# A two-layer hybrid attention trunk: the input projection with pairs of half-precision numbers in place of pairs of rounded single-precision ones

## The chip, the cores and the metric

One core of a Trainium2 chip runs the whole kernel in one launch. The metric is device time in microseconds (us). The matmul engine is called PE (PEld is its loading of weights), VectorE is DVE, ScalarE is ACT, GpSimd is POOL, and SP is the engine that issues most DMAs; DVE, ACT and POOL also work on the data between the matmuls. Each engine runs its instructions in order and waits for other engines by semaphores.

## What is computed

Two layers act on 512 latent tokens and 256 context tokens of 1024 features. Each layer normalizes and modulates its input (scale and shift come from a small projection of `c`), multiplies it by one wide matrix `w_in`, and takes ten pieces from the product:

```python
hx = _rmsnorm(x, norm_g) * (1.0 + scale_x) + shift_x
px = hx @ w_in                       # 1024 -> 5376 columns
a_k, a_v, b_k, b_v, a_q, b_q, a_z, b_z, g_a, g_b = _split(px, SPLIT_SIZES)
# widths      512  512  128  128  512  512  512  512 1024 1024
a_att = _na_latent(rmsnorm(a_q), rmsnorm(a_k), a_v, context k and v, rpb)  # neighbourhood attention
b_att = grouped attention of rope(rmsnorm(b_q)), rope(rmsnorm(b_k)), b_v
o_a = (a_att * silu(a_z)) @ w_o_a ;  o_b = (b_att * silu(b_z)) @ w_o_b
x = x + gate_x * ((sigmoid(g_a) * o_a + sigmoid(g_b) * o_b) @ w_out)
```

The norms of q and k go over heads of 64 columns and add `EPS` to the mean of squares. The context passes through the same weights in layer 0; in layer 1 only its k and v are needed. All data are float32. The change touches `hx @ w_in` and what scales its ten pieces.

## The kernel before

**Products of pairs.** A float32 matmul is made of three. Each factor is split into a high half, rounded to the format `fp32r` (4 bytes an element), and a low half, the rest; `mm3` (line 431) adds hi·hi, hi·lo and lo·hi in PSUM. The weights are split when they are loaded. `load_w` (395) takes 512 columns in eight raw tiles of 128 rows: for each an SP DMA of 256 KB into one of three "raw" buffers, a cast by ACT (403) into a "whi" buffer, and a subtraction (406) by POOL or DVE into a "wlo" buffer; there are eight buffers of each kind, and for AQ and half of BQ some of the attention's own. `load_w2` (410) does the same for 256 columns, with two blocks of 128 rows in a tile, so four tiles (cast 418, subtraction 420). `mix_lo` and `bq_lo` (425, 426) say whose the subtraction is: `mix_lo` gives POOL the even tiles and DVE the odd ones. So a tile's cast waits only for its own DMA, and its subtraction only for its cast. The input `hx` lies turned (features on the partitions) as hi and lo, made by `start_mod` (374) for layer 0 and `make_hx`/`turn_hx` (324, 335) for layer 1, during layer 0's output projection.

**Order of the work.** A layer is written as a sequence of stages, and PE follows that order: AK, AV and AQ (`tok_proj`, 443: tokens on the partitions, eight steps of three matmuls of 128x512 for each of six or four blocks of 128 tokens); then neighbourhood attention, head by head; then BKV (256 columns) and BQ; grouped attention; the branches' products with `w_o_a` and `w_o_b` and their merge; the output projection (1205 to 1240). The remaining projections (`a_z`, `b_z`, `g_a`, `g_b`) are cut into twelve chunks of 256 columns (`fill_chunks`, 607; `chan_proj`, 450: features on the partitions). Their loads and pieces are put between the heads of the attentions (`pipeline`, 997), where PE would wait for the softmax, two loads ahead of their use (`in_order`, 630). What a chunk gives is evacuated by ACT's tanh (614), DVE's product for silu (616), and partly spilled to memory by DMA (618). A stage's weights are loaded and split while the stage before computes; the framework's scheduler settles each engine's order from the dependences and the order of the program.

**Evacuation.** `evac_na` (543) squares and sums a block by heads (`head_ss`, 497, with `EPS` in an extra column that `open_heads`, 490, writes), takes the power -1/2 on POOL (`head_pow`, 503), multiplies, and `turn` (520) transposes the result on PE a little later. Transposes go to PSUM buffers of kind "t", of which there are two. `evac_va` (558) splits V again. `head_out` (789) and `divide` (806) add the two halves of an attention's output and multiply it by the silu gate. `stage_q` (849) lays a head's queries out in the attention's own "qs" buffers.

Of the kernel before, what the change touches and what calls it, by code (L numbers as in the profile page):

```python
# [44 lines left out]
XB, RX = 6, 2  # L45

# [24 lines left out]
def hybrid_kernel(es: ExitStack, tc, x, ctx, cvec, w_ada, w_ada0, small, gvec, w_in, w_o_a, w_o_b, w_out,  # L71
# [72 lines left out]
    hx0 = [[big("hx") for _ in range(2)] for _ in range(2)]  # L144
# [26 lines left out]
    def raw_tile():  # L171
        return wp.tile([128, 512], F32, tag="raw", name=nm("raw"), bufs=3)
# [134 lines left out]
    def ada_mod(l):  # L307
        mod_finish(l, ada_sum(0, 16, 2).rearrange("p (a k) v -> p a k v", a=2), 0, 8)

# [25 lines left out]
    def turn_hx(l, t, y, h, hx, pool):  # L335

        v = 0 if t < 4 else 1
        full = pool.tile([128, 4, 128], F32, tag="half", name=nm("half"), bufs=2)
        pt = psw(512, "t")
        for k in range(4):  # L340
            T.transpose(pt[:, 128 * k:128 * k + 128], y[:, 512 * h + 128 * k:512 * h + 128 * k + 128], ident)
        for k in range(4):
            kk = 4 * h + k
            S.activation(full[:, k, :], pt[:, 128 * k:128 * k + 128], AF.Identity,
                         bias=modc[:, l, v, kk:kk + 1], scale=modc[:, l, v, 8 + kk:9 + kk])
        hi = hx[0][h].rearrange("p (k n) -> p k n", k=4)[:, :, 128 * t:128 * t + 128]
        lo = hx[1][h].rearrange("p (k n) -> p k n", k=4)[:, :, 128 * t:128 * t + 128]
        V.tensor_copy(R(hi), full)
        V.tensor_tensor(R(lo), full, hi, ALU.subtract)
# [34 lines left out]

    def split_hi(raw):
        hi = wp.tile([128, 512], F32R, tag="whi", name=nm("whi"), bufs=8)
        S.copy(hi, raw)
        return hi

    def split_lo(raw, hi, eng):  # L390
        lo = wp.tile([128, 512], F32R, tag="wlo", name=nm("wlo"), bufs=8)
        eng.tensor_tensor(lo, raw, F(hi), ALU.subtract)
        return hi, lo

    def load_w(src, col0, n, nk, lo_eng, k0=0, own=None, bufs=8):

        pool, x = (wp, "") if own is None else (own, "x")
        res = []
        for k in range(k0, k0 + nk):
            raw = raw_tile()  # L400
            nc.sync.dma_start(raw[:, :n], src[128 * k:128 * k + 128, col0:col0 + n])
            hi = pool.tile([128, 512], F32R, tag="whi" + x, name=nm("whi"), bufs=bufs)
            S.copy(hi[:, :n], raw[:, :n])  # L403
            lo = pool.tile([128, 512], F32R, tag="wlo" + x, name=nm("wlo"), bufs=bufs)
            e = lo_eng(k)
            e.tensor_tensor(lo[:, :n], raw[:, :n], F(hi[:, :n]), ALU.subtract)  # L406
            res.append((hi, lo))
        return res

    def load_w2(src, col0, nk, lo_eng):  # L410

        res = []
        for i in range(nk // 2):
            raw = raw_tile()
            nc.sync.dma_start(raw.rearrange("p (k n) -> p k n", k=2),
                              src[256 * i:256 * i + 256, col0:col0 + 256].rearrange("(k p) n -> p k n", k=2))
            hi = wp.tile([128, 512], F32R, tag="whi", name=nm("whi"), bufs=8)
            S.copy(hi, raw)  # L418
            lo = wp.tile([128, 512], F32R, tag="wlo", name=nm("wlo"), bufs=8)
            lo_eng(i).tensor_tensor(lo, raw, F(hi), ALU.subtract)  # L420
            res += [(hi[:, c:c + 256], lo[:, c:c + 256]) for c in (0, 256)]
        return res

# [4 lines left out]
    def hx_k(hx, part, k):  # L428
        return hx[part][k // 4].rearrange("p (k n) -> p k n", k=4)[:, k % 4, :]
# [6 lines left out]

    def tok_mm(ps, w, n, a, t, k0, k1):
        for k in range(k0, k1):
            hi, lo = a(0, k), a(1, k)
            mm3(ps, (R(hi[:, 128 * t:128 * t + 128]), R(lo[:, 128 * t:128 * t + 128])),  # L440
                (w[k][0][:, :n], w[k][1][:, :n]), k == 0, k == KT - 1)
# [8 lines left out]
    def chan_proj(w, f, a, n0, n1, evac, late=0):  # L450


        ps = psw(n1 - n0)
        nk = len(w)
        wh = lambda k, i: w[k][i][:, 128 * f:128 * f + 128]
        act = lambda k, i: R(a(i, k)[:, n0:n1])
# [9 lines left out]
    hp = {"late": [], "lag": 0}  # L466

# [22 lines left out]
    def open_heads(stack, name, bufs):  # L490

        hp["p"] = stack.enter_context(tc.tile_pool(name=name, bufs=bufs, reuse_waits="tile"))
        hp["sq"] = [hp["p"].tile([128, 8, HD + 1], F32, name=nm("sq"), bufs=1) for _ in range(2)]
        for sq in hp["sq"]:
            V.memset(sq[:, :, HD:HD + 1], HD * EPS)

# [87 lines left out]
    def layer(l, hx, nxt, start):  # L584
# [3 lines left out]
        a_hx = lambda part, k: hx_k(hx, part, k)  # L588
# [17 lines left out]

        def fill_chunks(col0, dst, spill, silu, eng):

            def evac(f, n0, n1, ps):
# [4 lines left out]
                S.activation(d, ps, AF.Tanh, scale=0.5)  # L614
                if silu:
                    V.scalar_tensor_tensor(d, d, 1.0, ps, ALU.add, ALU.mult)
                if spill is not None:
                    (nc.sync if not first else G if silu else S).dma_start(spill[:, f, n0:n1], d)
            res = []
            for i in range(2):  # L620
                st = {}

                def ld(i=i, st=st):
                    st["w"] = load_w2(W, col0 + 256 * i, KT, eng)
                res.append((ld, [lambda f=f, n0=n0, n1=n1, i=i, st=st:
                                 chan_proj(st["w"], f, a_hx, n0, n1, lambda f, a, b, ps: evac(2 * i + f, a, b, ps))
                                 for f in range(2) for n0, n1 in spans]))
            return res
# [64 lines left out]

        bgp_es = ExitStack()
# [25 lines left out]
        else:  # L720
            open_heads(bgp_es, f"cp{l}", 1)
            w = load_w(W, C_AK, 512, KT, mix_lo)
# [18 lines left out]
        w = load_w(W, C_AQ, 512, KT, mix_lo, own=hp["p"])  # L741
# [17 lines left out]
        if True:  # L759
# [29 lines left out]
            def head_out(po, e, dst, eng=None):  # L789
# [3 lines left out]
                t1 = att["p"].tile([128, 512], F32, tag="ho", name=nm("ho"), bufs=1)  # L793
                a = t1[m:m + 64, :n]
                S.copy(a, po[o:o + 64, :n])
                V.tensor_tensor(a, po[m:m + 64, :n], a, ALU.add)
# [52 lines left out]
            def stage_q(src, e):  # L849

                n = 768 if first else 512
                qs = att["p"].tile([128, n], F32R, tag=f"qs{e}", name=nm("qs"), bufs=1)
# [35 lines left out]
            def ctx_values(p, vsl, dst, e, back=None):  # L888
# [18 lines left out]
                head_out(po, e, dst)  # L907
# [7 lines left out]
            def open_att(name, width, n_p, n_t):  # L915
# [3 lines left out]
                att["turn"], att["spare"] = 0, False  # L919
# [10 lines left out]
            V.memset(bedg[64:128, 0:128], NEG)  # L930

# [36 lines left out]
            def na_values(h, ps_):  # L968
# [25 lines left out]
                head_out(po, e, zv[64 * e:64 * e + 64, h // 2, 0:512], V if h == 7 else G)  # L994
# [21 lines left out]
            akt = [k_tile(e, True) for e in range(2)]  # L1016

# [8 lines left out]
            def values_of(dst, f, back=None):  # L1026
                def g(h, st):
                    vsl = f(h, st[0])
                    if first:
                        e = h % 2  # L1030
                        zv = dst.rearrange("p (f n) -> p f n", f=4)
                        ctx_values(st[1], vsl, zv[64 * e:64 * e + 64, h // 2, 512:768], e, back)
# [39 lines left out]
            def split_vb():  # L1072
                shrink(vf.rearrange("p t n -> p (t n)"), vs, vbig[:, 2946:2948], vbig[0:1, 2948:2949])
                v = vf.rearrange("p t (h d) -> p (t h) d", h=2)
                d = vb.rearrange("p t h q d -> p (t h) q d")
                S.activation(d[:, :, 0, :], v, AF.Copy, scale=vs[:, 0:1])
# [4 lines left out]
            w = load_w2(W, C_BKV, KT, mix_lo)  # L1081
            w_q = load_w(W, C_BQ, 512, 4, bq_lo) + load_w(W, C_BQ, 512, 4, bq_lo, 4, hp["p"], 4)
# [11 lines left out]
            def evac_bq(t, ps):  # L1094
# [3 lines left out]
                else:  # L1098
                    rope_heads(4, ps, rs, gbc[:, 0, :], None, qbv, t)
            for t in range(qt):  # L1100
# [19 lines left out]
            lift = vbig[:, 2950:2951].to_broadcast([128, 768])  # L1120

# [15 lines left out]
            def gq_values(h, st):  # L1137
# [6 lines left out]
                divide(psw(512, "t"), r, e, dst, vs[:, 1:2])  # L1144
# [30 lines left out]
            pipeline(fill, 8, gq_first, values_of(zb, gq_values, vs[:, 1:2]), early, bg)  # L1175
            gq_es.close()

        with tc.tile_pool(name=f"mrg{l}", bufs=1, reuse_waits="tile") as mp:
# [37 lines left out]
            for n in range(2):  # L1216
# [200 lines left out]
    hx1 = []  # L1417

    def nxt():
        if not hx1:  # L1420
            hx1.extend([[big("hx") for _ in range(2)] for _ in range(2)])
# [78 lines left out]
```

## Time and profile before

| | us |
|---|---|
| median of 3 runs (lowest, highest) | 1127.27 (1126.77, 1128.93) |
| the profiled execution | 1127.56 |
| its span, first to last instruction | 1125.6 |
| granted TensorE clock over the span | 0.993 |
| PE busy, 5826 instruction records | 1093.3 |
| ACT busy | 579.0 |
| DVE busy | 774.7 |
| POOL busy | 490.6 |

The spans of the stages, read from the timeline (us from the start of the span; edges to a few us, since a stage's evacuation runs into the next):

| | start and AK | AV | AQ | neighb. att. | BKV, BQ | grouped att. | merge | out |
|---|---|---|---|---|---|---|---|---|
| layer 0 | 0-63 | 63-102 | 102-133 | 133-306 | 306-382 | 382-550 | 550-592 | 592-659 |
| layer 1 | 659-692 | 692-727 | 727-753 | 753-881 | 881-938 | 938-1050 | 1050-1075 | 1075-1126 |

How to read the rows that follow: a group's row gives the line, engine and operation, out<-in by the program's names, the shape (partitions x elements) and type, how often, busy us and the mean ns of one, and the idle time of the engine ahead of them with what ended it. A timeline row gives start and duration in us. PE's matmuls are pipelined: a duration holds the way through the array too, and consecutive starts are closer together than durations.

### The profile page before, as it was taken

To read this page: it belongs to the slowest core of one execution; us is meant where nothing else is said; L and a number is where in the kernel's file an instruction comes from. 1 tells how busy PE (TensorE), PEld (TensorE's weight loads), DVE (VectorE), ACT (ScalarE), POOL (GpSimd) and SP (SyncE) were. 2 spreads that over 40 slices of the span, in tenths; PEclk is the share of its full clock that TensorE was granted. 3 is DMA by queue.
4 is the path that set the end of the run, shared out by engine and by line. 5 is a ranking of instruction groups with operands and counts; after the bars stand their busy time and mean duration, and the time that the engine had idled before them with its cause. 6 is when DMAs were issued, how large, how long until landed. Compare 5 with 4: busy or idle time off the path is not lost.

```text
span 1125.6 us, 16862 instructions
## 1 busy us (share of the span) xinstructions
PE 1093.3 (97%) x5826; PEld 905.3 (80%) x5826; DVE 774.7 (69%) x1492; ACT 579.0 (51%) x1154; POOL 490.6 (44%) x405
## 2 busy tenths in 40 slices
PE   8999999999999999979999999999999999999998
PEld 5688888888998877757788888888888987776677
DVE  4666788897466477776577785458878765677473
ACT  6453266665433576755330284326666446776431
POOL 1054254654247144454521545235554563563531
PEclk9999999999999999989999999999999999999999
DMA  9454322242351488869633532553333236989742
GB/s 373 143 172 140 114 63 66 73 136 89 93 168 38 123 201 185 185 172 269 173 108 125 183 129 72 142 174 92 100 107 116 59 105 172 188 224 239 197 145 80
DMA packets 192222, 161.29 MB, mean 143 GB/s; under 512 B 116364, under 2 KB 158088, under 8 KB 190472
## 3 DMA queue, kind: packets, MB, share of 16 engines
q1 hardware_dynamic: 184800, 145.82, 46.8%
q0 software_dynamic: 2368, 7.87, 2.1%
q10 hardware_dynamic: 4968, 6.53, 1.7%
q8 instruction: 46, 0.75, 0.3%
q14 instruction: 40, 0.33, 0.1%
HBM read 115.58 MB, written 17.32 MB: 118 GB/s over the span
## 4 chain that ended last, share of the span: by engine, by line
PE 38%; issue 4%; DVE 3%; DMA 3%; POOL 2%; ACT 1%; SPq 1%; POOLq 0%; ACTq 0%
PE psx L435 6%; PE psx L433 6%; PE psx L434 6%; PE psf L433 4%; PE psf L434 4%; PE psf L435 4%; PE pss L955 1%; PE pss L861 1%; POOL wlo L406 1%; PE pss L862 1%; PE pst L779 1%; PE pst L1148 1%; DMA raw<-in_w_o_a_dram 1%; PE pst L1149 1%; DMA raw<-in_w_in_dram 1%
## 5 line engine op out<-in xcount | busy, mean ns | idle before, releaser
L420 POOL TENSOR_TENSOR wlo<-raw,whi 128x512 fp32r<-128x512 f32 x70 | 97.9, 1405 | 106.1 <-ACT whi L418 70.4
L433 PE MATMUL psf<-hx,whi 128*128 128x512 f32 (+1 forms) x360 | 138.0, 383 | 3.2 <-ACT zt L614 2.4
L435 PE MATMUL psf<-hx,wlo 128*128 128x512 f32 (+1 forms) x360 | 135.8, 377 | 0.0
L434 PE MATMUL psf<-hx,whi 128*128 128x512 f32 (+1 forms) x360 | 135.1, 375 | 0.0
L433 PE MATMUL psx<-whi,hx 128*128 128x512 f32 (+1 forms) x328 | 120.8, 372 | 0.0
L434 PE MATMUL psx<-wlo,hx 128*128 128x512 f32 (+1 forms) x328 | 119.6, 366 | 0.0
L435 PE MATMUL psx<-whi,hx 128*128 128x512 f32 (+1 forms) x328 | 119.5, 365 | 0.0
L418 ACT CAST whi<-raw 128x512 fp32r<-128x512 f32 x136 | 82.3, 620 | 64.0 <-DMA raw<-in_w_in_dram 35.3
L406 POOL TENSOR_TENSOR wlo<-raw,whi 128x512 fp32r<-128x512 f32 x40 | 61.2, 1535 | 122.1 <-ACT whi L403 80.1
L803 POOL TENSOR_TENSOR h<-p,h 128x768 f16<-128x768 f32 (+1 forms) x40 | 65.7, 1644 | 96.4 <-ACT h L802 72.0
L403 ACT CAST whi<-raw 128x512 fp32r<-128x512 f32 x88 | 54.1, 623 | 99.2 <-PE psx L435 34.2
L420 DVE TENSOR_TENSOR wlo<-raw,whi 128x512 fp32r<-128x512 f32 x66 | 73.6, 1115 | 30.6 <-ACT whi L418 29.0
L504 POOL TENSOR_TENSOR ss<-ss,ehalf 128x8 f32<-128x8 f32 (+2 forms) x40 | 62.5, 1566 | 72.9 <-DVE ss L501 72.8
L433 PEld LDWEIGHTS psf<-hx,whi 128*128 128x128 f32 x360 | 67.9, 188 | 15.4 <-ACT zt L614 3.7
L435 PEld LDWEIGHTS psf<-hx,wlo 128*128 128x128 f32 x360 | 67.8, 188 | 11.6
L1131 DVE CUSTOM_DVE_ANT_0 p<-pss,vb 128x768 f32<-128x768 f32 x64 | 60.3, 953 | 23.6 <-PE pss L862 21.1
L434 PEld LDWEIGHTS psf<-hx,whi 128*128 128x128 f32 x360 | 67.9, 189 | 10.3
L1132 ACT ACTIVATE p<-pss,mx 128x768 f32<-128x768 f32 x64 | 57.6, 900 | 34.7 <-DVE mx L1131 33.7
L435 PEld LDWEIGHTS psx<-whi,hx 128*128 128x128 f32 x328 | 61.9, 189 | 10.0
L434 PEld LDWEIGHTS psx<-wlo,hx 128*128 128x128 f32 x328 | 62.0, 189 | 9.2
L433 PEld LDWEIGHTS psx<-whi,hx 128*128 128x128 f32 x328 | 61.8, 189 | 8.9
L435 PE MATMUL psx<-hx,wlo 128*128 128x256 f32 (+1 forms) x208 | 68.0, 327 | 0.0
(362 smaller groups left out, 3095.8 us busy)
## 6 DMA issues: line engine op xcount, KB each, us to landing
raw<-in_w_in_dram SPq DMA_DIRECT2D x168, 256.0 KB, 2.9
rawb<-in_w_ada_dram SPq DMA_DIRECT2D x48, 256.0 KB, 2.8
raw<-in_w_out_dram SPq DMA_DIRECT2D x32, 256.0 KB, 2.9
tg<-gs SPq DMA_DIRECT2D x4, 1536.0 KB, 6.8
rawx<-in_w_ada_dram SPq DMA_DIRECT2D x4, 1024.0 KB, 9.8
rawy<-in_w_ada_dram SPq DMA_DIRECT2D x4, 1024.0 KB, 9.5
gs<-zt ACTq DMA_DIRECT2D x16, 256.0 KB, 2.0
raw<-in_w_o_a_dram SPq DMA_DIRECT2D x16, 256.0 KB, 3.4
```

What stands on the lines that cost most here:

```text
L403: S.copy(hi[:, :n], raw[:, :n])
L406: e.tensor_tensor(lo[:, :n], raw[:, :n], F(hi[:, :n]), ALU.subtract)
L418: S.copy(hi, raw)
L420: lo_eng(i).tensor_tensor(lo, raw, F(hi), ALU.subtract)
L433: T.matmul(ps, lhs[0], rhs[0], start=first, stop=False)
L434: T.matmul(ps, lhs[0], rhs[1], start=False, stop=False)
L435: T.matmul(ps, lhs[1], rhs[0], start=False, stop=last)
L504: G.tensor_tensor(ss, ss, ehalf[:, :n], ALU.pow)
L779: T.transpose(pt[:, c0:c0 + 128], src, ident)
L803: eng.tensor_tensor(h[:, 1], p[:, :n], h[:, 0], ALU.subtract)
L1131: V.tensor_tensor_reduce(p, pss, lift, -1.0, 3e38, ALU.add, ALU.min, mx[:, 0:1])
L1132: S.activation(p, pss, AF.Exp, bias=mx[:, 0:1], accum_out=r[:, i:i + 1])
```

## The change

The weights and the input of `hx @ w_in` become pairs of float16 numbers, hi and lo, which `mm3` multiplies as before. Layer 0's AK (in the kernel's start) and AV stay as they were; layer 0's AQ, BKV, BQ and twelve chunks, and all of layer 1's input projections, change. Since float16 has a narrow range, both factors are scaled.

- **The weights' scale** is found on the chip for each load (`load_h`). ACT squares each raw tile with a sum along the row; then `up_scale` adds the tiles' sums on DVE, sums over the partitions with a 128x1 matmul against a constant `ones`, limits the result on DVE, and raises it to -1/2 on POOL. Only then are the tiles converted. A tile whose low half is DVE's: ACT scales raw into hi, DVE makes raw·b - hi in one instruction. A tile whose low half is POOL's: ACT scales raw in place, ACT casts it to hi, POOL subtracts.
- **The input's scale** `xa[l]` comes in the same way from the modulation's scales and shifts (`x_scale`). In layer 1 it is multiplied into the modulation, so that `turn_hx` writes halves. In layer 0 `half_x` makes pairs from the single-precision input, two of eight pieces after each block of AV (ACT a scaled copy of 128x768, DVE the rest), with one DMA to move a piece that needed a spare place.
- **Undoing the scales.** `head_eps` multiplies `EPS` in the norms of q and k by the scale squared. The tanh of a chunk takes its scale from `sc`. The factor of the silu gates and of V is applied later, as an operand in `head_out` and `divide` (tiles `zcs`, `backs`).
- **Buffers.** Five raw tiles in place of three. One kind of weight buffer, "w", 16 of them: a single-precision pair takes two, a half-precision pair one. The queries of `stage_q` move to one big tile, and layer 1's grouped attention finds another place for the tile of `head_out`.
- **Layer 1's AK weights** are loaded and converted in layer 0's output projection, at its second half's second block (`load_ahead`), into two big tiles, no longer at the start of layer 1.

```diff
+    def up_scale(ss, n, scale, pt=None):
+        one = sp.tile([128, 1], BF16, tag="one", name=nm("one"), bufs=2)
...
+                V.tensor_reduce(one, ss[:, :n], AX, ALU.add)
+        if pt is None:
+            pt = psw(512, "t")
+        T.matmul(pt[:, 0:1], ones.to_broadcast([128, 128]), one, start=True, stop=True)
+        V.tensor_scalar(scale, pt[:, 0:1], 1.0e-37, None, ALU.max)
+        G.tensor_tensor(scale, scale, ehalf[:, 0:1], ALU.pow)
...
+    def load_h(l, src, col0, n, lo_eng, own=None, place=None):
+        res, raws, slots = [], [], []
+        nt = 8 * n // 512
+        ss = sp.tile([128, 8], F32, tag="wss", name=nm("wss"), bufs=2)
+        for i in range(nt):
...
+                raw = raw_tile()
...
+                nc.sync.dma_start(raw, src[128 * i:128 * i + 128, col0:col0 + n])
...
+            S.activation(slot.bitcast(BF16)[:, 0:512], raw, AF.Square, accum_out=ss[:, i:i + 1])
...
+        up_scale(ss, nt, b)
+        G.tensor_tensor(ab, b, xa[l], ALU.mult)
+        V.reciprocal(c, ab)
+        G.tensor_scalar(ch, c, 0.5, None, ALU.mult)
+        for i in range(nt):
+            raw, hi, lo = raws[i], slots[i][:, 0:512], slots[i][:, 512:1024]
+            e = lo_eng(i)
+            if e is V:
+                S.activation(hi, raw, AF.Copy, scale=b)
+                V.scalar_tensor_tensor(lo, raw, b, hi, ALU.mult, ALU.subtract)
+            else:
+                S.activation(raw, raw, AF.Copy, scale=b)
+                S.copy(hi, raw)
+                e.tensor_tensor(lo, raw, hi, ALU.subtract)
...
+            def one(k):
+                src = yT[k // 4].rearrange("p (k n) -> p k n", k=4)[:, k % 4]
+                S.activation(at[k][:, 0], src, AF.Copy, scale=xa[0])
+                V.scalar_tensor_tensor(at[k][:, 1], src, xa[0], at[k][:, 0], ALU.mult, ALU.subtract)
...
-            w = load_w(W, C_AK, 512, KT, mix_lo)
+            w, sc = ahead.pop() if half else load_in(C_AK, 512, mix_lo)
...
-        w = load_w(W, C_AV, 512, KT, mix_lo)
+        if first and half:
+            w = load_w(W, C_AV, 512, KT, mix_lo)
+            x_scale(0)
+            to_half = half_x()
+        else:
+            w, sc = load_in(C_AV, 512, mix_lo, hp["p"] if half else None)
...
         for t in range(6):
             tok_proj(w, 512, a_hx, t, evac_va(va))
+            run(to_half, 2)
...
-        w = load_w(W, C_AQ, 512, KT, mix_lo, own=hp["p"])
+        w, sc = load_in(C_AQ, 512, mix_lo, hp["p"], place=({}, None) if first else None)
+        if half:
+            head_eps(sc)
...
-            w = load_w2(W, C_BKV, KT, mix_lo)
-            w_q = load_w(W, C_BQ, 512, 4, bq_lo) + load_w(W, C_BQ, 512, 4, bq_lo, 4, hp["p"], 4)
+            w, sc_kv = load_in(C_BKV, 256, mix_lo)
+            w_q, sc_q = load_in(C_BQ, 512, bq_lo, hp["p"], hp["p"])
+            if half:
+                head_eps(sc_kv)
...
+                    if first and n == 1 and t == AHEAD_T and HALF[1]:
+                        ahead.append(load_ahead())
                     tok_proj(w, 512, a_m, t, evac_o)
```

More of the change, by code (lines that the diff above doesn't have):

```diff
@@ L740, in layer @@
         qav = big("qa").rearrange("p (j n) -> p j n", j=4)
-        w = load_w(W, C_AQ, 512, KT, mix_lo, own=hp["p"])
+        if first and half:
+            run(to_half, len(to_half))
+            hx_now[0] = hx16
+        w, sc = load_in(C_AQ, 512, mix_lo, hp["p"], place=({}, None) if first else None)
+        if half:
+            head_eps(sc)
         za = big("za")
@@ L1016, in layer @@
             akt = [k_tile(e, True) for e in range(2)]
+            backs = sp.tile([128, 2, 2], F32, tag="backs", name=nm("backs"), bufs=1)
+            back_a = lambda h: backs[:, 0, h // 4:h // 4 + 1] if half else None
+            if half:
+                for j in range(2):
+                    if first:
+                        G.tensor_copy(backs[:, 0, j:j + 1], zc[0][j])
+                    else:
+                        G.tensor_tensor(backs[:, 0, j:j + 1], zc[0][j], zcs[:, 4], ALU.mult)
             def na_first(h):
@@ L1099, in evac_bq @@
                     rope_heads(4, ps, rs, gbc[:, 0, :], None, qbv, t)
+            if half:
+                head_eps(sc_q)
+            back_b = lambda h: backs[:, 1, h // 4:h // 4 + 1] if half else vs[:, 1:2]
             for t in range(qt):
```

189 lines of the change are left out of this document (152 added, 37 removed).

## The prediction

> **What bounds the kernel now.** I read the page first: the engines' busy shares, then the 40 slices.
>
> ```profile
> span 1125.6 us, 16862 instructions
> PE 1093.3 (97%) x5826; PEld 905.3 (80%) x5826; DVE 774.7 (69%) x1492; ACT 579.0 (51%) x1154; POOL 490.6 (44%) x405
> PE   8999999999999999979999999999999999999998
> PEclk9999999999999999989999999999999999999999
> ```
>
> PE (TensorE matmul) works 97% of the span, and in all slices but a few at nine tenths or more, at full clock. So PE's stream of matmuls sets the end: what shortens a matmul comes off the time, and what makes PE wait goes on top. All else is hidden unless it makes PE wait. The second view is the windows by stage (start:end and length; PE, PEld, DVE, ACT and POOL busy with their counts; granted clock, DMA share, GB/s). In order: layer 0's AV and AQ projections, its BKV and BQ projections, its grouped attention; then layer 1's AV, AQ, neighbourhood attention, BKV and BQ, and grouped attention.
>
> ```profile
> 63.00:102.00 39.00, 39.00 (x181) 32.33 (x180) 25.40 (x42) 19.23 (x35) 20.63 (x11) 1.00 0.45 129
> 102.00:133.00 31.00, 31.00 (x148) 25.51 (x148) 22.91 (x55) 8.25 (x16) 11.13 (x7) 1.00 0.45 136
> 306.00:382.00 76.00, 76.00 (x444) 66.51 (x443) 42.29 (x76) 29.88 (x61) 37.87 (x31) 1.00 0.35 110
> 382.00:550.00 168.00, 153.11 (x850) 122.05 (x849) 115.96 (x207) 105.09 (x203) 75.97 (x54) 0.97 0.80 187
> 592.00:659.00 67.00, 66.92 (x305) 55.25 (x304) 53.04 (x116) 19.10 (x40) 24.77 (x34) 1.00 0.45 149
> 692.00:727.00 35.00, 35.00 (x163) 29.08 (x162) 15.04 (x25) 15.80 (x27) 14.52 (x11) 1.00 0.49 142
> 727.00:753.00 26.00, 26.00 (x122) 21.38 (x121) 14.14 (x30) 7.77 (x14) 9.32 (x7) 1.00 0.64 189
> 753.00:881.00 128.00, 126.71 (x679) 107.84 (x677) 105.48 (x207) 81.67 (x166) 65.53 (x62) 1.00 0.32 97
> 881.00:938.00 57.00, 56.35 (x315) 48.48 (x316) 38.98 (x69) 24.97 (x53) 34.39 (x28) 1.00 0.32 99
> 938.00:1050.00 112.00, 107.91 (x512) 81.55 (x511) 78.14 (x127) 82.34 (x147) 56.97 (x38) 1.00 0.93 212
> ```
>
> In the projections (AV, AQ, BKV, BQ) PE has no gap at all, though each begins with weights that were loaded and converted for it: the conversion is done before the stage begins. Only the grouped attentions leave PE idle for more than a few per cent.
>
> **The matmuls.** They are issued back to back, so the distance between starts is the price, not the duration shown. Timeline rows of PE, the first and the last of a run of one kind without other rows between:
>
> ```profile
> 704.20 0.39 PE L433 MATMUL psx<-whi,hx 128*128 128x512 f32 x1
> ...
> 705.56 0.39 PE L433 MATMUL psx<-whi,hx 128*128 128x512 f32 x1
> 303.99 0.28 PE L435 MATMUL psx<-hx,wlo 128*128 128x256 f32 x1
> ...
> 304.59 0.28 PE L434 MATMUL psx<-hx,whi 128*128 128x256 f32 x1
> 508.04 0.38 PE L1149 MATMUL pst<-ht,vb 128*128 128x512 f16 x1
> ...
> 509.12 0.38 PE L1148 MATMUL pst<-ht,vb 128*128 128x512 f16 x1
> 522.80 0.61 PE L896 MATMUL psv<-ct,vb 128*128 128x256 f16 x4
> L896 PE MATMUL psv<-ct,vb x16: 272/273/283, 426.6 to 549.1; 128*128 128x256 f16 x16
> ```
>
> Rounded single precision (f32 rows): 1.36/6 = 227 ns for 512 columns, 0.60/5 = 120 ns for 256. Half precision: 1.08/5 = 216 ns for 512, and (0.61 - 0.273)/3 = 112 ns for 256. So a pair product gets 11 ns cheaper at 512 columns and 8 (to 11) ns at 256. By the loops, 1920 matmuls of 512 columns are converted (layer 0: AQ 144, chunks 576, BQ 144; layer 1: AK 144, AV 144, AQ 96, chunks 576, BQ 96) and 864 of 256 (layer 0: chunks 576, BKV 144; layer 1: BKV 144). Layer 0's AK and AV stay as they are, and so do the output projections. 1920 x 11 + 864 x 8 ns = 21.1 + 6.9 = **-28 us** (-24 if only half of the 256-column gain comes, -31 with the most of it).
>
> **The sums of squares.** Each converted load now squares its raw tiles on ACT, sums over its columns on DVE, sums over partitions by a 128x1 matmul with `ones`, takes a power on POOL, and only then can ACT make the first half. The rows nearest to each step:
>
> ```profile
> L418 ACT CAST whi<-raw 128x512 fp32r<-128x512 f32 x136 | 82.3, 620 | 64.0 <-DMA raw<-in_w_in_dram 35.3 <-DMA raw<-in_w_o_a_dram 8.6 <-PE psf L434 6.7
> L500 ACT ACTIVATE sq<-y 128x512 f32<-128x512 f32 x6 | 3.7, 630 | 0.0
> L961 ACT ACTIVATION_READ_ACCUMULATOR p<-p,mx 128x1 f32 x64 | 12.1, 189 | 0.0
> L823 PE MATMUL pst<-ident,vb x4: 245/255/265, 340.7 to 912.8; 1*128 1x1 f32 x4
> L824 DVE TENSOR_SCALAR vb<-pst x2: 145/146/146, 342.1 to 915.2; 128x1 f32<-128x1 f32 x2
> L361 POOL TENSOR_TENSOR ss<-ss,ehalf x6: 550/553/865, 6.1 to 22.1; 128x1 f32<-128x1 f32 x6
> ```
>
> ACT: 152 raw tiles (68 in layer 0, 84 in layer 1) get a Square and an accumulator read, 0.63 + 0.19 = 0.82 us, 125 us in all; the 72 tiles whose low half POOL makes get a scaling ahead of their cast, 72 x 0.62 = 45. ACT goes from 579 to about 750 us, 65% of the new time: still not the bound on average. PE: 34 added 128x1 matmuls; each costs some 0.12 us of issue, nothing if they slip between others, 0.255 at most: **+4 us** (0 to 8.7).
>
> What matters is where these matmuls stand in PE's order. The order of instructions in the changed kernel as it is built, at layer 0's AQ (number, line, operation, out<-in):
>
> ```text
> PE  356 L524 Matmult psx_168_990<-whi_140_762,hx_7_99 128x512
> PE  358 L451 Matmult pst_193_1064<-one_192_1062,ones_154 128x1 [waits Activation_49]
> PE  360 L522 Matmult psf_220_1173<-wh_176_1031,yT_9_101 128x512 [waits Activation_49]
> ACT 103 L502 raw_175   104 L499 wh_178   105 L502 raw_179   106 L499 wh_182
> ACT 107 L502 raw_183   108 L499 wh_186   109 L502 raw_187   110 L499 wh_190   111 L503 wh_176
> ```
>
> The last product of AV, then the sum over partitions, then the first product of AQ. Engines run in order, so the sum isn't taken until AV is through, and the first product needs `wh_176`, whose cast stands on ACT behind eight scalings: PE has nothing to do meanwhile. (The sum's PSUM tile is of the two-buffer "t" kind, which the evacuations of the stage before use.) The chain: matmul 0.255 + DVE 0.146 + POOL 0.553 = 0.95, with some 0.1 for each of four hand-overs 1.4 us (estimated from these rows; 0.95 at least); then nine ACT operations at 0.62, 5.6 us: 7.0 us. The same order stands at layer 1's AV and AQ. BKV loads four tiles of 256 columns twice, so five operations: 1.4 + 3.1 = 4.5 us, in both layers. Sum 3 x 7.0 + 2 x 4.5 = **+30 us**; these stalls take the place of no wait, as there was none. Bounds: 2 us each, 10 us, if only the chain up to POOL and one cast count; 37 if DVE or POOL, with low halves of 1.1 to 1.5 us in hand when the sum comes, hold each chain up by a little over one of these.
>
> **The clock.** What such a gap does besides, one place of this trace shows, in layer 0's grouped attention:
>
> ```profile
> 495.93 0.41 PE L862 MATMUL pss<-gk,qs 128*128 128x256 f32 x1
> 502.15 0.69 PE L811 MATMUL psv<-ident,r 128*128 128x128 f32 x2 [5.80 <-DVE ho L796]
> 506.05 0.63 PE L433 MATMUL psf<-gah,whi 128*128 128x512 f32 x1
> 506.87 0.40 PE L435 MATMUL psf<-gah,wlo 128*128 128x512 f32 x1
> 500.00:504.00 4.00, 1.85 (x7) 1.66 (x8) 3.09 (x6) 0.00 (x0) 1.83 (x2) 0.50 0.14 31
> ```
>
> After 5.8 us without work the granted clock is 0.50, matmuls take 0.63 in place of 0.40 until 506.8: 4.7 us at half speed, 2.3 us lost. Five stalls of 4.5 to 7 us: 5 x 2.3 = **+11.5 us** (0 if none is long enough, 17 if each loses half as much again). The Trainium skill (TensorE: Matmul & The Clock Gate, Part 1: The HAM clock gate) says that the clock halves after an idle window of about 3.4 us that runs free of the kernel, and comes back after a busy one; the trace agrees for its 5.8 us gap. By that rule a gap of 4.5 us need not hold a whole window, so that the two BKV starts could escape: the sum would be some 4 us less.
>
> **Loads inside the attentions.** The 24 chunks load while PE has other work, so the order decides: between the `ones` matmul and the first use of its weights stand, by PE's order and the distances above, 4.8 to 35 us of products in layer 0, but in layer 1 6.3, 3.0, 5.8, 2.8 and 9.4 (neighbourhood) and 6.9, 1.7 and 10.6 us (grouped). Against the 4.5 us chain three are short, by 1.5, 1.7 and 2.8: **+6 us** (0 if chains are quicker by a third; 15 if ACT, busy with exponentials, delays each chunk of the attentions by a further 0.5 us or so).
>
> **Costed at nothing**, with the cover. Half pairs of layer 0's input: eight ACT and eight DVE operations of 128x768 in the AV stage (rows below, 7.5 and 9.8 us), where ACT is busy 19 and DVE 25 of 39 us; without room they would go on AQ's start. One more DMA on SP. Low halves: a half-precision POOL one is 1.22 us against 1.41, DVE's fused one of 768 is 1.23, of 512 less than today's 1.12, so these engines gain. Layer 1's AK load, 8 DMAs of 256 KB, moves on SP's queue ahead of the out projection's last loads, at a DMA share of 0.45 (row 592 to 659): the last loads come at most some us later, and cost it if PE is waiting. Five raw buffers for three let a load's DMAs run ahead, but a raw tile is now held until its sum: with chunks of four, the next chunk's second DMA waits on SP, and bias and spill reloads behind it; they have a whole head's time. The scales (`head_eps`, `zcs`, `backs`, about 1.7 us of POOL for each load) lie on POOL at 44%. The tanh scale and V's factors are operands of instructions that exist.
>
> ```profile
> L1076 ACT ACTIVATE vb<-vf,vb 128x768 f16<-128x768 f32 x2 | 1.9, 936 | 0.1
> L1078 DVE SCALAR_TENSOR_TENSOR vb<-vf,vb x2: 1225/1228/1231, 343.5 to 916.5; 128x768 f16<-128x768 f32 x2
> L420 DVE TENSOR_TENSOR wlo<-raw,whi 128x512 fp32r<-128x512 f32 x66 | 73.6, 1115 | 30.6 <-ACT whi L418 29.0 <-PE psf L435 1.0
> L420 POOL TENSOR_TENSOR wlo<-raw,whi 128x512 fp32r<-128x512 f32 x70 | 97.9, 1405 | 106.1 <-ACT whi L418 70.4 <-PE psx L434 12.7 <-PE psf L434 12.0
> L803 POOL TENSOR_TENSOR h<-p,h 128x512 f16<-128x512 f32 x8 | 9.8, 1219 | 6.7 <-issue 4.7 <-ACT h L802 1.9
> ```
>
> **Sum**, against the profiled execution's own 1127.6 us (1125.6 span and 2.0 around it; 0.3 over the median of the runs): 1127.6 - 28 + 4 + 30 + 11.5 + 6 = **1151 us**.
>
> **The rivals.**
> - *Faster: short starts.* The matmuls gain as said, but a stage start costs PE only 2 us (ACT's scalings quicker than its casts, or PE far enough behind that the sum is taken early), too short for the clock to drop: 1127.6 - 28 + 4 + 10 + 2 = 1116. It decides below (28 - 4)/5 = 4.8 us for a start, clock included. For it: half-width outputs, and PE idle in no projection now. Against it: the in-order position of `ones` and the eight scalings ahead of the first cast.
> - *ACT becomes the bound in the attentions.* A chunk puts 4 x 0.82 + 2 x 0.62 = 4.5 us on ACT, in front of the exponentials that PE waits for. ACT has 105 of 168 and 82 of 112 us in hand in the grouped attentions; three or four chunks in each bring the latter to 96 or 100 of 112. If each of the 24 chunks holds PE up by 1 us more: +24, 1175. Against it: ACT is free for a quarter of every stage.
> - *The matmuls get no faster* (the spacing of pairs set by weight loads or by PSUM, not by the type): 1151 + 28 = 1179. Against it: the half-precision rows above, which load weights as often.
>
> **How the numbers follow.** My forecast (1131 to 1168) 0.65; short starts 0.15; a balance of gain and stalls within 0.2% (2.3 us, about what a measurement of this kernel can tell from no change) 0.05; ACT 0.12; matmuls no faster 0.03. Range 1118 to 1172: the forecast's own, half of short starts, and most of ACT's case; the bounds of all terms at once (1107 and 1181) are left out. Faster 0.15, same 0.05, slower 0.80.
>
> **What would show it right or wrong.** Right: spacing 216 and 112 ns in the converted products; at five stage starts a PE gap of 4.5 to 7 us put down to ACT's cast at the first product, with the clock at 0.5 behind it; PE's busy share down some per cent; ACT about 750 us. Wrong: no PE gap over 3 us at AQ or BKV; spacing still 227; PE waiting for ACT's exponentials in the attentions for over 20 us more.

## The result, and the profile after

The changed kernel takes 1198.4 us (median of 4 runs, 1195.0 to 1200.1) against 1127.0: 1.063 times as long (95% interval 1.060 to 1.066), **71 us slower**. The forecast had the sign and 24 of these us; 1198 lies 26 above its range. The profiled execution took 1199.0 us. Its page, the same rows as of before:

```profile
span 1197.2 us, 17386 instructions
PE 1100.3 (92%) x5860; PEld 726.9 (61%) x5860; DVE 782.7 (65%) x1601; ACT 737.9 (62%) x1542; POOL 526.0 (44%) x553
PE   8997999999899987988999897799798899899998
PEclk9998999999999998999999998899898899899999
```

PE has fallen from 97% to 92% of a longer span. It is *busier* in microseconds than before (1100 against 1093), though its products are shorter: part of them ran at half clock. The windows by stage (columns as before; layer 0's AQ, neighbourhood attention and BKV/BQ; layer 1's AK, AV, AQ, neighbourhood attention and BKV/BQ):

```profile
98.30:140.20 41.90, 35.44 (x168) 17.00 (x168) 24.22 (x60) 26.32 (x55) 23.62 (x29) 0.92 0.44 126
140.20:320.60 180.40, 171.91 (x1087) 116.66 (x1086) 140.44 (x314) 123.36 (x273) 84.49 (x91) 0.99 0.27 82
320.60:401.30 80.70, 74.84 (x449) 45.19 (x447) 44.51 (x94) 56.48 (x123) 46.30 (x59) 0.96 0.34 108
...
681.00:725.90 44.90, 39.82 (x202) 21.24 (x201) 25.35 (x44) 32.53 (x84) 15.56 (x15) 0.96 0.18 58
725.90:766.40 40.50, 32.77 (x146) 14.53 (x145) 11.37 (x24) 15.94 (x34) 7.42 (x10) 0.92 0.28 79
766.40:797.10 30.70, 23.46 (x105) 10.46 (x103) 13.74 (x34) 19.12 (x39) 15.41 (x22) 0.89 0.46 129
797.10:939.50 142.40, 129.60 (x668) 78.42 (x666) 103.06 (x225) 105.12 (x224) 70.29 (x82) 0.95 0.27 80
939.50:1013.20 73.70, 65.56 (x367) 37.24 (x365) 42.00 (x87) 51.54 (x116) 41.99 (x55) 0.93 0.37 112
```

Each projection stage that had no idle time now has 6 to 8 us, and its clock is below 1. But layer 1's neighbourhood attention is 14 us longer too, in pieces. The waits of PE (engine, tile and line that waits, what it waits for; us in total, times, longest) name two kinds:

```profile
PE psx L522 <- ACT wh L503: 18.1, 4, 7.7
PE psf L522 <- ACT wh L503: 18.1, 6, 6.5
PE pss L1029 <- ACT p L1325: 7.6, 6, 3.4
PE pst L348 <- ACT half L351: 4.5, 1, 4.5
PE pst L936 <- DVE ptl L945: 4.0, 3, 2.3
...
PE psv L1152 <- ACT pth L944: 3.1, 1, 3.1
```

36 us for ACT's casts of weights (L503; 29 of them at five stage starts, 7 inside the attentions), and many small ones for steps of the softmax and for the turning of layer 1's input, which hardly waited before.

To add this up, take each matmul's distance to the next in both traces, less its own issue time (216 and 109 ns in half, 227 and 120 ns in single precision; below), and split the rest into what the granted clock explains and true idle time. The split is good to 2 or 3 us, since stages have no sharp edges and a few matmuls lack a record:

| us, after less before | products | half clock | idle |
|---|---|---|---|
| whole span | -31 | +26 | +77 |
| the five stages that begin with a sum (AQ, BKV/BQ; AV, AQ, BKV/BQ) | -5 | +12 | +36 |
| both neighbourhood attentions | -14 | +6 | +29 |
| layer 0's out projection and AK of layer 1 | -1 | +1.5 | +7 |
| the rest | -11 | +6.5 | +5 |

### The profile page after: what moved, and what is told of

The parts are those of the page before. It is cut to its first block, busy times and chain, and to the rows that moved or that the text cites. A ratio compares the mean times of both kernels' runs of the same rounds, so it can differ in the third digit from the quotient of the medians.

```text
span 1197.2 us, 17386 instructions
## 1 busy us (share of the span) xinstructions
PE 1100.3 (92%) x5860; PEld 726.9 (61%) x5860; DVE 782.7 (65%) x1601; ACT 737.9 (62%) x1542; POOL 526.0 (44%) x553
## 5 line engine op out<-in xcount | busy, mean ns | idle before, releaser
L486 ACT ACTIVATE wh<-raw 128x512 bf16<-128x512 f32 x144 | 90.1, 627 | 60.8 <-DMA raw<-in_w_in_dram 60.2
L504 POOL TENSOR_TENSOR wh<-raw,wh 128x512 f16<-128x512 f32 x68 | 85.6, 1276 | 47.0 <-ACT wh L503 37.6
L522 PE MATMUL psf<-yT,wh 128*128 128x512 f16 (+1 forms) x240 | 87.1, 363 | 4.3 <-DVE zt L740 1.6
L522 PEld LDWEIGHTS <-wh 128*128 128x128 f16 x576 | 57.3, 100 | 55.5 <-ACT wh L503 8.8
L523 PEld LDWEIGHTS <-wh 128*128 128x128 f16 x576 | 57.3, 100 | 51.0 <-issue 13.3
L524 PE MATMUL psf<-yT,wh 128*128 128x512 f16 (+1 forms) x240 | 86.8, 362 | 0.1
L523 PE MATMUL psf<-yT,wh 128*128 128x512 f16 (+1 forms) x240 | 86.8, 362 | 0.0
L500 DVE SCALAR_TENSOR_TENSOR wh<-raw,wsc,wh 128x512 f16<-128x512 f32 x76 | 74.2, 994 | 17.7 <-ACT wh L499 17.3
L524 PEld LDWEIGHTS <-wh 128*128 128x128 f16 x576 | 57.3, 99 | 46.4 <-issue 5.4
L420 POOL TENSOR_TENSOR wlo<-raw,whi 128x512 fp32r<-128x512 f32 x20 | 28.5, 1429 | 94.0 <-ACT whi L419 86.7
L1324 DVE CUSTOM_DVE_ANT_0 p<-pss,vb 128x768 f32<-128x768 f32 x64 | 60.2, 951 | 12.8 <-PE pss L1030 11.5
L1029 PE MATMUL pss<-gk,qs 128*128 128x256 f32 (+1 forms) x144 | 54.3, 383 | 10.2 <-ACT p L1325 7.6
L419 ACT CAST whi<-raw 128x512 fp32r<-128x512 f32 x40 | 24.6, 619 | 56.4 <-PE psx L523 42.6
L967 ACT CAST h<-p 128x768 f16<-128x768 f32 (+1 forms) x72 | 57.4, 807 | 2.4 <-DMA ht<-h 1.5
L523 PE MATMUL psx<-wlo,mh 128*128 128x512 f32 (+1 forms) x144 | 54.2, 380 | 0.2 <-DVE wlo L420 0.2
## 6 DMA issues: line engine op xcount, KB each, us to landing
rawy<-in_w_ada_dram SPq DMA_DIRECT2D x4, 1024.0 KB, 10.7
```

Source lines behind the costliest of these rows:

```text
L486: S.activation(slot.bitcast(BF16)[:, 0:512], raw, AF.Square, accum_out=ss[:, i:i + 1])
L500: V.scalar_tensor_tensor(lo, raw, b, hi, ALU.mult, ALU.subtract)
L504: e.tensor_tensor(lo, raw, hi, ALU.subtract)
L522: T.matmul(ps, lhs[0], rhs[0], start=first, stop=False)
L523: T.matmul(ps, lhs[0], rhs[1], start=False, stop=False)
L524: T.matmul(ps, lhs[1], rhs[0], start=False, stop=last)
```

## A stage start, read row by row

Layer 0's AQ, PE and ACT from the timeline (start, duration), and a window just behind it, with its clock of 0.50:

```profile
98.13 0.39 PE L524 MATMUL psx<-whi,hx 128*128 128x512 f32 x1
98.36 0.18 PE L451 MATMUL pst<-one,ones 128*128 128x1 bf16 x1
99.41 0.72 ACT L502 ACTIVATE raw<-raw,wsc 128x512 f32<-128x512 f32 x1 [0.28 <-POOL wsc L453]
...
103.72 0.71 ACT L499 ACTIVATE wh<-raw,wsc 128x512 f16<-128x512 f32 x1
104.33 1.65 ACT L503 CAST wh<-raw 128x512 f16<-128x512 f32 x3
104.99 0.58 PE L522 MATMUL psf<-wh,yT 128*128 128x512 f16 x1 [6.46 <-ACT wh L503]
```

```profile
106.00:109.00 3.00, 3.00 (x9) 1.03 (x7) 0.00 (x0) 1.73 (x5) 3.00 (x4) 0.50 0.48 107
```

The sum on PE at 98.36, ACT's first scaling 1.05 us later, eight scalings 0.61 apart, the first cast, then PE: 6.6 us, for which 7.0 was forecast. The five starts come to 6.6, 7.9 and 7.4 (loads of eight tiles), and 4.6 (in two pieces) and 4.2 (BKV), 30.7 together. Farther on, the products run as forecast:

```profile
109.79 0.38 PE L524 MATMUL psx<-wh,yT 128*128 128x512 f16 x1
...
111.94 0.38 PE L522 MATMUL psx<-wh,yT 128*128 128x512 f16 x1
208.58 0.27 PE L522 MATMUL psx<-yT,wh 128*128 128x256 f16 x1
...
209.78 0.27 PE L524 MATMUL psx<-yT,wh 128*128 128x256 f16 x1
```

2.15/10 = 215 ns and 1.20/11 = 109 ns.

## The experiments

Theory: the wait for a sum that PE's order holds back costs the time. Rivals: ACT's load; the edits costed at nothing. The kernel before took 1126.5 to 1127.1 in each comparison. The first four take the chain of sums apart.

**No sums, a constant scale.**

```diff
-            S.activation(slot.bitcast(BF16)[:, 0:512], raw, AF.Square, accum_out=ss[:, i:i + 1])
...
-        up_scale(ss, nt, b)
+        G.memset(b, 512.0)
```

> The half-precision pairs stay; what finds the weights' scale on the chip is left out (no squares, no sums; the scale is a constant 512). Both theories (that conversions wait for a sum which stands late in PE's order, or that ACT is overloaded by squares) expect the nominal gain of the matmuls, 31.5 us, and no gap at the stage starts: 1127 - 31 + 0 to 8 = 1096 to 1104 us. If the pairs themselves cost something (the input's conversion, the buffers, the factors undone later), over 1115.

Measured 1132.0 (1.0047, interval 1.0030 to 1.0064). The stage-start gaps are gone and the products have their gain (-31 us in this trace too), yet the time is *over* that of before: 36 us of loss have nothing to do with the weights' sums. The third answer of the expectation holds, the theory covers only the 66 us above.

**Squares taken, not used.** The Square stays, its sum has no reader.

```diff
-        up_scale(ss, nt, b)
+        G.memset(b, 512.0)
```

> As the constant-scale kernel, but ACT squares every raw tile again (144 Squares with their accumulator reads, about 118 us of ACT); the sums are not taken further and nothing waits for them. Theory 1, the wait for the sum is the cost: 0 to 10 us over the constant scale, 1100 to 1112. Theory 2, ACT's load is what stalls the attentions: 35 to 50 us over it, 1135 to 1150.

1137.9: 6 us more, while ACT's busy time on the page rises by 85 us (645.9 to 730.5; 118 were expected). What ACT's load costs by itself is small.

**Sums taken, not awaited.**

```diff
-        up_scale(ss, nt, b)
+        G.memset(b, 512.0)
+        up_scale(ss, nt, ss[:, 0:1])
```

> As the kernel with unused squares, and the sums are taken through to the power (DVE reduce, 128x1 matmul with ones, limit, power on POOL), but the conversions use the constant and don't wait. Theory 1: the 34 matmuls cost PE only their issue and a few waits, 4 to 10 us over the unused squares. A rival, that the matmul itself makes PE wait for late sums (squares wait for DMA): 30 us or more over it.

1141.7, 4 us more: the matmuls with `ones` cost what was forecast (+4). What is left to the changed kernel, 1198.4 - 1141.7 = 57 us, is the conversions' wait.

**No sum over partitions.**

```diff
-        T.matmul(pt[:, 0:1], ones.to_broadcast([128, 128]), one, start=True, stop=True)
-        V.tensor_scalar(scale, pt[:, 0:1], 1.0e-37, None, ALU.max)
+        V.tensor_scalar(scale, one, 128.0 * X_UP ** -2, 1.0e-37, ALU.mult, ALU.max)
```

> The whole chain as in the changed kernel, and the conversions wait for it, but the sum over partitions on PE is left out (each partition's own sum is scaled up in its place), so the chain is off PE. Theory 1 as I priced it (PE's order holds the sum back to the stage's join): the stage starts' 36 us of idle and about 10 of clock go, 1198 - 46 = 1152, and the attentions' part goes too where it comes from the same order, down to 1115. If the chain is slow by itself (all raw tiles of a load must land and be squared before the first conversion), it stays over 1175.

1152.6 (1148.2 to 1157.1): 46 of the 57 us (41 to 50 by this spread) go when the chain leaves PE, though all else still waits for it. Since the matmuls and their PSUM tiles cost only 4 us where nothing awaits them, the step's place in PE's order is shown as the cause of most of the wait. What the other 11 us are made of was not tested. One gap in this kernel's trace, at layer 1's AV, tells of another queue:

```profile
698.21 0.15 DVE L449 TENSOR_SCALAR wsc<-one 128x1 f32<-128x1 bf16 x1
...
701.36 0.56 POOL L450 TENSOR_TENSOR wsc<-wsc,ehalf 128x1 f32<-128x1 f32 x1
...
707.51 1.01 PE L519 MATMUL psx<-wh,hx 128*128 128x512 f16 x2 [6.22 <-ACT wh L500]
```

The power on POOL begins 3 us after DVE's step, behind POOL's powers for the norms of AK, and ACT's eight scalings follow it.

**Where the wait is paid.** Constant scales (and no squares) for one kind of load only; `fixed` is `col0 >= C_AZ` in the first kernel and `col0 < C_AZ` in the second.

```diff
-        up_scale(ss, nt, b)
+        if fixed:
+            G.memset(b, 512.0)
+        else:
+            up_scale(ss, nt, b)
```

> The changed kernel with a constant scale for the 24 chunk loads alone (no squares and sums for them); the nine loads of AK, AV, AQ, BKV and BQ keep the whole chain. By my forecast's term for loads inside the attentions, 6 us, and the squares' cost: 1185 to 1192. By the idle time in the trace (34 us more in the attentions than before, 8 in the constant-scale kernel) with its share of the clock: 1155 to 1165.

> The complement: constant scale for the loads of AK, AV, AQ, BKV and BQ, the whole chain for the 24 chunks. By my forecast (30 of stalls and 11.5 of clock at the starts): 1198 - 42 = 1156; by the trace (36 of idle, 12 of clock there): 1150. If the two kinds are independent, this and the kernel with fixed chunks together take off what the constant-scale kernel takes off, 66 us.

Chunks fixed: 1179.3, 19 us less, three times the forecast's term, and less than the trace's idle time promised. Starts fixed (these are eight loads, not nine): 1163.0, 35 less, where 42 and 48 were expected. Together 54 of the 66 us; 12 go only when both go.

What a chunk's wait does is seen in layer 1's neighbourhood attention (timeline):

```profile
900.55 0.49 PE L938 MATMUL pst<-ident,p 128*128 128x128 f32 x3
900.92 0.72 ACT L502 ACTIVATE raw<-raw,wsc 128x512 f32<-128x512 f32 x1
...
902.77 0.71 ACT L499 ACTIVATE wh<-raw,wsc 128x512 f16<-128x512 f32 x1
903.50 1.07 ACT L944 CAST pth<-pst 128x512 fp32r<-128x512 f32 x2
904.14 0.63 PE L1152 MATMUL psv<-pth,va 128*128 128x512 f32 x1 [3.10 <-ACT pth L944]
```

PE has turned the probabilities by 901.0. Their cast on ACT (L944) stands behind four scalings of a chunk. PE waits 3.1 us, not for weights at all. This is one gap; that the other small ones have the same cause was not followed one by one.

**Conversions in the program's order on ACT.**

```diff
-            if e is V:
+            def conv(raw=raw, hi=hi, lo=lo, e=e):
...
+            behind(ON_ACT, conv)
```

> The changed kernel with everything it does, but on ACT each load's conversions keep the program's order, so that the first tile's cast stands behind one scaling, not behind eight (or four). Theory 1 (PE waits at the stage starts through ACT's scalings): the five gaps of 7 us shrink by about 4 us at loads of eight tiles and 1.5 at loads of four, 3 x 4 + 2 x 1.5 = 15, and the clock falls less (5 to 10): 1198 - 20 to 25 = 1173 to 1178. If the gaps come from the sum alone: within 5 us of 1198.

1186.9: 11.5 less, half of the expected. In its trace the three long starts lose about 4 us of idle time each, as computed; but by the same split of PE's time layer 0's neighbourhood attention now has some 7 us more of idle time and 6 of half clock. ACT's order is part of the cause at the starts, and a better order there is paid for elsewhere.

**The edits that were costed at nothing.** First, beside the weights' constant, the input's:

```diff
+    for l in range(2):
+        G.memset(xa[l], 4.0)
...
-            x_scale(l)
...
-            x_scale(0)
```

> The constant-scale kernel (1132.0 us) with the input's scale a constant too (4 for both layers): the squares and the sum over the modulation are left out. In that kernel's trace PE waits 6.6 us for the sum's first step and 3.8 behind it in layer 0's output projection, with 3 us of half clock after it. If these belong to the input's sum: 1132 - 13 = 1119, faster than before by 8. If the loads of layer 1's AK, which stand there as well, are the cause: 1128 to 1132.

1134.9, no gain (3 us over the constant weights' scale alone): the gap that I laid to the input's sum stays. Its rows in this kernel show another cause:

```profile
658.43 0.72 ACT L502 ACTIVATE raw<-raw,wsc 128x512 f32<-128x512 f32 x1 [4.93 <-DMA raw<-in_w_in_dram]
659.06 2.88 ACT L350 ACTIVATE half<-pst,modc 128x128 f32<-128x128 f32 x8
660.60 1.12 PE L347 MATMUL pst<-ident,y 128*128 128x128 f32 x4 [7.54 <-ACT half L350]
```

ACT stands 4.9 us before a tile of AK's weights that hasn't landed; the modulation of layer 1's input (L350) is behind it, and PE behind that.

> Both scales constant, five raw buffers, and layer 1's AK weights loaded at the start of layer 1 as before the change. If the eight tiles that are converted in layer 0's output projection hold up the modulation and turning of layer 1's input there: 3 to 6 us under the kernel with both scales constant. If they are hidden there: the same or up to 3 us slower.

```diff
-            w, sc = ahead.pop() if half else load_in(C_AK, 512, mix_lo)
+            w, sc = load_in(C_AK, 512, mix_lo)
...
-                    if first and n == 1 and t == AHEAD_T and HALF[1]:
+                    if False:
```

1124.1 (0.9975 of before, 0.9966 to 0.9985): 10.7 us less, more than the 3 to 6 expected. The early load was not free.

> Both scales constant, and three raw buffers as before the change in place of five. If loads that run further ahead put their low halves on DVE in front of the rope and the norms (PE waits for DVE's rope in BKV and BQ, 7 to 9 us), three buffers take that back: 8 us under the same kernel with five. If the pacing of loads doesn't matter: within 3 us of it. If five buffers hide waits: slower than it.

```diff
-RAW, W_SLOTS = 5, 16
+RAW, W_SLOTS = 3, 16
```

1132.8 against 1134.9: three buffers gain 2 us of the 8 expected, within the 3 us that were to mean no effect. My idea of loads that run too far ahead falls.

**Plain pairs.** The kernel before with its fp32r pairs replaced by float16 pairs, and nothing else:

```diff
+            if half:
+                hi = H(hi, 512)
             S.copy(hi[:, :n], raw[:, :n])
...
-            e.tensor_tensor(lo[:, :n], raw[:, :n], F(hi[:, :n]), ALU.subtract)
+            e.tensor_tensor(lo[:, :n], raw[:, :n], hi[:, :n] if half else F(hi[:, :n]), ALU.subtract)
```

> The kernel before, with no more changed than the type of the input projection's pairs: weights and input are split into float16 hi and lo as they were split into fp32r, by the same instructions on the same engines, with no scales, no sums, no held raw tiles, no early load of AK, and three raw buffers; layer 0's AK and AV are halves as well. The numbers have less range, nothing else is left out. It tells where the gain went in the constant-scale kernels (29 us short of 1127 - 32 with AK loaded in place). If their added work (double conversions on ACT, the input's second conversion, the EPS and back factors) eats it: 1127 - 32 - 3 (for AK and AV) = 1092, at most 1100. If PE's shorter products run into the evacuation chains on DVE and ACT, whatever is converted: 1110 to 1124.

1100.4 (0.9774 of before, 0.9760 to 0.9787), **the fastest of all**, 26 us under the kernel before. Its page:

```profile
PE 1056.9 (96%) x5826; PEld 691.5 (63%) x5826; DVE 770.6 (70%) x1492; ACT 576.2 (52%) x1154; POOL 480.2 (44%) x405
```

PE's busy time is 36 us less than before, ACT's nearly the same, and PE still works 96% of the span. So the gain of the type is real, but not all of it arrives: 26 of some 34 us (31, and 3 for AK and AV). By the same split PE's idle time is 7 us more than before, in many pieces; their causes stay open. The 24 us up to 1124.1 must then be added work, and two more kernels take it apart:

```diff
-            if e is V:
-                S.activation(hi, raw, AF.Copy, scale=b)
-                V.scalar_tensor_tensor(lo, raw, b, hi, ALU.mult, ALU.subtract)
-            else:
-                S.activation(raw, raw, AF.Copy, scale=b)
-                S.copy(hi, raw)
-                e.tensor_tensor(lo, raw, hi, ALU.subtract)
+            S.copy(hi, raw)
+            e.tensor_tensor(lo, raw, hi, ALU.subtract)
```

> The kernel with both scales constant and AK in place (1124.1 us), the weights' scale set to 1 and the conversions as before the change: one cast on ACT and one subtraction on POOL or DVE for each tile, so 72 ACT operations of 0.62 to 0.71 us less. If the doubled conversions are what is lost against plain pairs (1100.4): 1104 to 1112. If they are hidden: 1120 to 1124.

```diff
-        G.tensor_tensor(ab, b, xa[l], ALU.mult)
-        V.reciprocal(c, ab)
-        G.tensor_scalar(ch, c, 0.5, None, ALU.mult)
...
-                S.activation(d, ps, AF.Tanh, scale=0.5 if sc is None else sc[:, 2:3])
+                S.activation(d, ps, AF.Tanh, scale=0.5)
...
-            back_b = lambda h: backs[:, 1, h // 4:h // 4 + 1] if half else vs[:, 1:2]
+            back_b = lambda h: vs[:, 1:2]
```

> As the kernel with single conversions, and both scales 1, so that all that undoes them is left out: the scaled EPS of the norms, the factors of the silu gates and of V, the tanh scale, and their small operations on POOL and DVE. If these hold up the chains that PE waits for (the norms' sums wait for EPS): 6 to 12 us under the kernel with single conversions. If they are hidden: within 3 us of it.

1109.8 and 1109.8: the scaled and doubled conversions, with DVE's fused form, cost 14.3 us, the factors nothing. In the groups of ACT of the kernel with both scales constant and AK in place, the added one is the middle row:

```profile
L499 ACT ACTIVATE wh<-raw,wsc 128x512 f16<-128x512 f32 x80 | 57.8, 726 | 19.2 <-DMA raw<-in_w_in_dram 18.8
L502 ACT ACTIVATE raw<-raw,wsc 128x512 f32<-128x512 f32 x72 | 51.7, 724 | 78.3 <-DMA raw<-in_w_in_dram 59.8 <-POOL wsc L491 8.2 <-issue 4.0
L503 ACT CAST wh<-raw 128x512 f16<-128x512 f32 x72 | 44.5, 618 | 2.5 <-PE psx L524 2.1
```

A scaled operation takes 0.72 us, where the prediction's row of a plain cast had 0.62. In all ACT is busy 51 us more than with single conversions (643.7 against 592.9), and at 57% of the span it still costs the kernel 14. Of the last 9 us to the plain pairs, 3 are AK and AV of layer 0, in single precision there. Between these two traces layer 0's AQ loses 6 to 7 more: in the single-conversion kernel PE waits 3.7 us there for DVE, and the clock falls. The rows of DVE, ACT and PE:

```profile
115.89 0.62 ACT L498 CAST wh<-raw 128x512 f16<-128x512 f32 x1 [0.59 <-DMA raw<-in_w_in_dram]
116.54 0.69 DVE L499 TENSOR_TENSOR wh<-raw,wh 128x512 f16<-128x512 f32 x1 [2.19 <-ACT wh L498]
117.15 0.68 DVE L617 TENSOR_TENSOR y<-psf,ss 128x512 f32<-128x512 f32 x1
117.98 1.08 PE L629 MATMUL pst<-ident,y 128*128 128x128 f32 x4 [3.73 <-DVE y L617]
```

The norm (L617), whose power POOL had ready at 115.1, stands on DVE behind the low half of a tile of weights; that waits for ACT's cast, and this for its DMA. The input's second conversion is not in the way: its last operation ended at 85.8. Why this tile came late was not tried.

The ladder, in us of the medians. Each cost holds for this order of the steps:

| step | time | step's cost |
|---|---|---|
| plain float16 pairs, no scales | 1100.4 | |
| + layer 0's AK, AV in single precision, its input converted in AV, buffers | 1109.8 | 9.3 |
| + factors that undo the scales | 1109.8 | 0.1 |
| + scaled, doubled conversions | 1124.1 | 14.3 |
| + AK loaded ahead | 1134.9 | 10.7 |
| + the input's sum | 1132.0 | -2.8 |
| + squares | 1137.9 | 5.9 |
| + sums, not awaited | 1141.7 | 3.8 |
| + the wait for them (the change) | 1198.4 | 56.7 |

## Why the prediction was right in sign and wrong in size

- **Matmuls, -28.** Right for the products: some -31, at 109 in place of 112 ns for 256 columns. But what shortens a matmul did not all come off the time, as the plain pairs show (26 of 34).
- **The `ones` matmuls, +4.** Right: 3.8.
- **The five starts, +30.** Right by the trace: 30.7 for all five. The kernel with fixed starts gives back 35 of the 41.5 forecast with the clock.
- **The clock, +11.5.** Mis-sized: +26. The starts' stages hold 12, as forecast; the rest are gaps mostly in the attentions, for which I had no term. My remark that the BKV starts might escape by the Trainium skill's idle window (TensorE: Matmul & The Clock Gate, Part 1: The HAM clock gate) was wrong: both lost the clock, though the 3.4 us before it fell held 0.8 and 1.3 us of PE's work.
- **Loads inside the attentions, +6.** Mis-sized: 19 by the kernel with fixed chunks, and 29 us of idle time in the two neighbourhood attentions by the trace. What I did count, a chunk's *own weights* coming late, is about right: PE waits some 7 us for them there. The step that failed was to ask for nothing else. A delayed sum frees four tiles at once, and their scalings can go in front of the softmax's casts. This is my second rival's mechanism; I had priced it (+24), and kept it out of the sum, and the range ends at 1172, under that rival's own 1175. It needs no full ACT: ACT was busy 105 of 142 us in layer 1's neighbourhood attention. It is not the exponentials alone either: PE's waits for them rose from 3.6 to 10.2 us, less than the 20 that I had named as a sign.
- **Costed at nothing.** The largest failure: 36 us between 1132.0 and 1127 - 31. Of them 14 are the scaled, doubled conversions (I had put them on an ACT "not the bound on average"), 11 the early AK load (I looked at SP's queue, and not at ACT, which waits in order for the DMA), 6 the wait in layer 0's AQ, and 8 the part of the products' gain that plain pairs don't bring either; the input's sum takes 3 off. Squares, of which I had counted the ACT time but no cost, are 6 more.

The sum was 1151, and 47 more were measured. Along the ladder the terms don't overlap: products -3, edits costed at nothing +36, squares +6, the `ones` matmuls 0, and the wait for the sums +9 (57 in place of 30 + 11.5 + 6 = 47.5). That makes 48. So the wait, which the prediction is about, was nearly right in all, though not in its parts; what it put at nothing is most of the miss.

## What to carry to other kernels

A free engine is not a free queue. Before an edit costs nothing, list what stands behind it on its engine, above all where it can wait for a DMA or for a value that comes late: on engines in order, one late value delays work that has nothing to do with it. A step through PE for a scalar is paid by PE's order, not by its 0.2 us. And the half of the change that pays (the type) can be tried without the half that costs (the scales). It then lacks the range that the scales were for; no run here shows how far inputs may go without them.

## What was not expected of the hardware

The clock falls after shorter gaps than supposed. Layer 0's grouped attention, PE rows and two windows of the changed kernel:

```profile
518.65 0.40 PE L522 MATMUL psf<-gah,whi 128*128 128x512 f32 x1
521.64 0.50 PE L1029 MATMUL pss<-gk,qs 128*128 128x512 f32 x1 [2.59 <-ACT p L1048]
```

```profile
518.66:522.07 3.41, 0.82 (x4) 0.39 (x3) 2.77 (x4) 1.47 (x5) 3.41 (x2) 1.00 1.01 399
522.10:525.50 3.40, 2.98 (x9) 1.87 (x7) 0.38 (x1) 0.51 (x2) 3.40 (x4) 0.50 1.05 417
```

2.6 us without work, and the clock is at 0.50 for the next 3.4. Over all 15 traces of this case, of gaps at full clock (counted past the start of the kernel) 11 of 66 between 1.5 and 2 us had half clock set in by 3.5 us after their end, 21 of 40 between 2 and 2.5, 20 of 26 between 2.5 and 3, and all 46 above 3. For the shorter ones another gap close by may have had its part. The Trainium skill (TensorE: Matmul & The Clock Gate, Part 1: The HAM clock gate) has an idle window of about 3.4 us. The half-clock stretches here do come in pieces of 3.4 us, but the 3.4 us ahead of this one were not empty: PE was busy for 0.82 of them.
